# Loading the tokens, the first modulation chunk and the first key weights in longer lines and another order, with a reordered chain to the first normed tokens

## Chip, cores and metric

The kernel runs on one core of a Trainium2 chip. The metric is the device time of one execution in microseconds, the median of three runs.

## What is computed

One layer of a hybrid backbone over 256 latent tokens `x` of 1,024 channels, beside 256 context tokens `ctx`. Two vectors, `c` and `c_ctx`, give each token set its own shift, scale and gate through one weight `mod_w`. Cut to what matters here:

```python
c_act, cctx_act = silu(c), silu(c_ctx)
mod_l = c_act @ mod_w + mod_b          # six parts of 1024: sh1, sc1, g1, sh2, sc2, g2
mod_c = cctx_act @ mod_w + mod_b
hl = rmsnorm(x, norm1_g) * (1 + sc1_l) + sh1_l
hc = rmsnorm(ctx, norm1_g) * (1 + sc1_c) + sh1_c
z_l, z_c = hl @ in_w + in_b, hc @ in_w + in_b      # split into ten parts, keys among them
y_l = (sigmoid(..) * conv_l + sigmoid(..) * attention_l + sigmoid(..) * rnn_l) @ out_w
x = x + g1_l * y_l
x = x + g2_l * moe(rmsnorm(x, norm2_g) * (1 + sc2_l) + sh2_l)     # 16 experts, 2 per token
```

## The kernel before

Channels lie on the partitions: `xl` holds the tokens as 128 partitions x 8 blocks of channels x 256 tokens, `xct` the context in the same way. The projections work in three matmuls per block (`mm3`, lines 68 to 70), a weight and a token block each split into a high and a low part: `wh*xh`, `wh*xl`, `wl*xh`. A weight is loaded into a `raw` tile, its high part made on ScalarE, its low part on VectorE (`split_parts`, lines 201 and 202, in the start; `split`, lines 73 and 74, later).

The start, which the change touches, comes before the first projection, that of the keys. Its steps:

- **Loads**, all from the SyncE queue (`load`, line 78) in program order. At most eight are on their way at a time, since they share eight semaphores. Order: the conditioning `cct`, eight pieces of the tokens and the context in turn (two channel blocks each, lines of 2 KB), the table of small vectors `vc`, then the first modulation chunk in two halves (`load_ma_half`, four loads each, lines of 512 B), with the first key weight `w_k` between the halves; then the next two modulation chunks and key weights.
- **Sums of squares.** ScalarE squares each channel block of the tokens and of the context (lines 244, 245, 371, 372); VectorE adds them up in `sqs`, a part of the tile `nrm` (line 373). Four matmuls with a column of ones make the sums over the partitions (`pst`, line 381).
- **Modulation.** A `Mod` takes one or two blocks of scale and shift: `products` (line 349: small matmuls `mps` of 32 rows over the eight channel blocks), `copy` (ScalarE, line 354), `turn` (line 359, `mpt`) and `finish` (VectorE, `modA` and `modB`, lines 364 and 366). The first chunk goes in two halves, `m0` and `m1`, one channel block each.
- **Root and spread.** `rsqrt` (lines 294 to 305) is ten small VectorE instructions on four columns; `spread` copies the result to 128 columns for each (`ex`, line 312) and transposes it on TensorE (`prs`, line 315), so that it lies along the tokens. ScalarE copies that to `rstd1` (line 389).
- **Normed blocks.** `Channels(k)` scales a block on VectorE (`xn`, line 409), adds the shift and rounds on ScalarE (`h`, line 414), and makes the low part on VectorE (line 418). The first block then meets the first key weight: `kps` (lines 68 to 70).

After it, a loop of three rounds takes two channel blocks a round: 48 key matmuls, the products of the next modulation chunk, the split of the next key weight. The instructions of TensorE, ScalarE and VectorE in this stretch run in the order in which they are written (`manual_schedule`); from there on a scheduler orders them by data. Later come the convolution, the recurrence and the attention, the output projection, the second norm with the router (`rsqrt` again) and the experts, whose weights stream in 512 KB pieces through `ew` tiles as buffers come free.

## Time and profile before

| | |
|---|---|
| median of three runs | 615.6 us (613.79 to 617.37) |
| profiled execution | 619.23 us, its span 617.5 us |
| TensorE busy | 582.8 us (94% of the span) |
| VectorE busy | 349.0 us (57%) |
| ScalarE busy | 259.8 us (42%) |
| GpSimd busy | 19.4 us (3%) |
| moved by DMA | 170.64 MB, mean 276 GB/s |
| granted TensorE clock, mean | 0.997 |

Busy shares are means over the whole span; TensorE's 94% hides that the first slice of the span has almost no work for it. A change in one stage is read from the rows of that stage: which wait ended last there, and what the engines did beside it.

### The profile page before, as it was taken

The numbers are of one execution on the slowest core, as the hardware profiler recorded it, in microseconds if no ns is written. First come the engines' busy times: TensorE is split into PE (matmuls) and PEld (weight loads), VectorE is DVE, ScalarE is ACT, GpSimd is POOL, SyncE is SP. The second block draws the span as 40 slices with busy tenths as digits, with TensorE's granted clock in tenths as the row PEclk, the third lists the DMA queues.
The fourth block names the chain that finished last, engine by engine and source line by source line (L and its number), as shares of the span: only waits on it lengthen the run. The fifth ranks groups of instructions, "written<-read, shape, count | busy, mean of one in ns | idle before, by whom it ended". The sixth has DMA issues, their size and how long they took to land. (4 is left out here: it accounts for less than half of the span.)

```text
span 617.5 us, 10619 instructions
## 1 busy us (share of the span) xinstructions
PE 582.8 (94%) x4127; PEld 408.8 (66%) x4127; DVE 349.0 (57%) x797; ACT 259.8 (42%) x456; POOL 19.4 (3%) x42
## 2 busy tenths in 40 slices
PE   1999989999999899999999988998999999989996
PEld 0789878768788877888899974335444434454364
DVE  4667989999758977988468554120222303132123
ACT  4345436664498855886645634212111211131101
POOL 0000000000000000102212010000000000000000
PEclk9999999999999999999999998999999999999999
DMA  8983965446763373658969875999999999969971
GB/s 253 374 338 114 310 232 170 137 137 186 263 233 103 111 266 102 206 204 331 318 218 368 291 229 218 372 365 394 407 374 407 408 407 409 409 200 411 408 302 68
DMA packets 51824, 170.64 MB, mean 276 GB/s; under 512 B 5664, under 2 KB 10016, under 8 KB 51744
## 3 DMA queue, kind: packets, MB, share of 16 engines
q1 hardware_dynamic: 46704, 151.26, 66.9%
q0 software_dynamic: 5040, 18.35, 8.5%
q8 instruction: 45, 0.74, 0.5%
q14 instruction: 35, 0.29, 0.1%
HBM read 168.54 MB, written 1.05 MB: 275 GB/s over the span
## 5 line engine op out<-in xcount | busy, mean ns | idle before, releaser
L1162 PE MATMUL ph<-ew,xg 128*64 128x512 f32 (+1 forms) x576 | 115.8, 548 | 1.9 <-issue 1.6
L73 ACT ACTIVATE w<-raw 128x1024 fp32r<-128x1024 f32 x68 | 71.8, 1057 | 67.9 <-DMA raw<-in_w_in 12.0
L74 DVE TENSOR_TENSOR w<-raw,w 128x1024 fp32r<-128x1024 f32 x68 | 82.9, 1219 | 24.1 <-ACT w L73 22.5
L1162 PEld LDWEIGHTS ph<-ew,xg 128*64 128x64 f32 x576 | 40.7, 137 | 65.4 <-issue 56.5
L70 PE MATMUL gps<-h,w 128*128 128x256 f32 x192 | 55.2, 288 | 1.1 <-DVE w L74 1.1
L68 PE MATMUL gps<-h,w 128*128 128x256 f32 x192 | 56.0, 292 | 0.4 <-DVE y L934 0.4
L69 PE MATMUL gps<-h,w 128*128 128x256 f32 x192 | 54.5, 284 | 0.0
L593 DVE SCALAR_TENSOR_TENSOR cacc<-up,vc,cacc 128x243 f32<-128x243 f32 (+14 forms) x120 | 52.1, 471 | 1.4 <-ACT cacc L585 0.7
L1183 PE MATMUL py<-ew,heT 128*64 128x512 f32 x224 | 49.6, 595 | 1.2 <-ACT heT L1178 0.8
L1171 DVE SCALAR_TENSOR_TENSOR he<-sl,gsl,ph 128x256 f32<-128x256 f32 x16 | 7.1, 478 | 75.9 <-PE ph L1162 74.9
L74 DVE TENSOR_TENSOR ys<-py,ys 128x512 fp32r<-128x512 f32 (+1 forms) x18 | 11.4, 632 | 58.0 <-ACT ys L73 58.0
L68 PEld LDWEIGHTS gps<-h,w 128*128 128x128 f32 x192 | 36.7, 191 | 4.1 <-issue 2.6
L70 PEld LDWEIGHTS gps<-h,w 128*128 128x128 f32 x192 | 36.7, 191 | 2.8 <-issue 1.5
L69 PEld LDWEIGHTS gps<-h,w 128*128 128x128 f32 x192 | 36.7, 191 | 0.9 <-issue 0.7
L1183 PEld LDWEIGHTS py<-ew,heT 128*64 128x64 f32 x224 | 15.5, 137 | 30.8 <-issue 25.7
L1201 DVE SCALAR_TENSOR_TENSOR xl<-scp,g,xl 128x256 f32<-128x256 f32 x72 | 29.2, 476 | 7.6 <-PE scp L1197 7.6
L73 ACT ACTIVATE ys<-py 128x512 fp32r<-128x512 f32 (+1 forms) x18 | 9.9, 550 | 50.5 <-PE py L1183 36.6
L1167 ACT ACTIVATE sl<-ph 128x512 f32<-128x512 f32 (+1 forms) x9 | 4.9, 550 | 61.1 <-PE ph L1162 38.2
L114 POOL DMA_DIRECT2D ew<-in_w_exp x31 | 16.6, 537 | 323.5 <-ACT pp L813 251.2
L1119 ACT ACTIVATE xg<-gps,b2m 128x256 f32<-128x256 f32 x32 | 13.4, 470 | 24.6 <-PE gps L1115 23.8
L349 PE MATMUL mps<-ma,cs 128*32 128x256 f32 (+1 forms) x160 | 10.1, 397 | 13.4 <-DMA ma<-in_mod_a 13.2
L1115 PEld LDWEIGHTS gps<-oh,hT 128*128 128x128 f32 x128 | 16.2, 194 | 6.8 <-issue 3.7
(358 smaller groups left out, 1313.1 us busy)
## 6 DMA issues: line engine op xcount, KB each, us to landing
ew<-in_w_exp SPq DMA_DIRECT2D x161, 512.0 KB, 10.2
raw<-in_w_in SPq DMA_DIRECT2D x40, 512.0 KB, 4.3
ew<-in_w_exp POOLq DMA_DIRECT2D x31, 512.0 KB, 7.8
raw<-in_mod_b SPq DMA_DIRECT2D x28, 512.0 KB, 4.1
ma<-in_mod_a SPq DMA_DIRECT2D x12, 512.0 KB, 10.1
raw<-in_w_br SPq DMA_DIRECT2D x12, 512.0 KB, 4.2
raw<-in_w_out SPq DMA_DIRECT2D x8, 512.0 KB, 7.7
ma<-in_mod_a SPq DMA_DIRECT2D x8, 256.0 KB, 6.8
```

What stands on the lines that cost most here:

```text
L68: pe.matmul(ps, wh, xh, start=start, stop=False, skip_group_check=True)
L69: pe.matmul(ps, wh, xl_, start=False, stop=False, skip_group_check=True)
L70: return pe.matmul(ps, wl, xh, start=False, stop=stop, skip_group_check=True)
L73: act.activation(hi, src, AF.Copy)
L74: dve.tensor_tensor(lo, src, r32(hi), op=ALU.subtract)
L114: queue.dma_start(t, w_exp[6 * p + 2 * i + s, :, 1024 * q:1024 * q + 1024])
L593: dve.scalar_tensor_tensor(cacc[:, b, i0:i1], up[:, b, i0 + o:i1 + o], half_d[:, b * 31 + j:b * 31 + j + 1], cacc[:, b, i0:i1], op0=ALU.mu ...
L1115: pe.matmul(ps[:, j, :], hT[i][t][:, k * 128:k * 128 + 128], oh[t], start=(j == 0 and t == 0 and i == 0), stop=(t == 1 and i == 1), skip_g ...
L1119: act.activation(place(k0 + j), ps[:, j, :], AF.Identity, bias=b2m[:, k0 + j:k0 + j + 1])
L1162: pe.matmul(ph[64 * s:64 * s + 64, cols], xg(k)[:, c:c + 64], w[:, at], start=k == 0 and not h, stop=k == KD - 1, skip_group_check=True)
L1183: pe.matmul(py[q][64 * s:64 * s + 64, :], heT[f // 2][:, f % 2, 64 * s:64 * s + 64], ew[p][2][f][s][:, q * 512:q * 512 + 512], start=f == ...
L1201: dve.scalar_tensor_tensor(xl[:, m, :], ps[:, j, :], g2[:, m:m + 1], xl[:, m, :], op0=ALU.mult, op1=ALU.add)
```

## The change

**Loads.** The tokens come in pieces of four channel blocks (lines of 4 KB, 512 KB each), the last half of the context in two pieces of two blocks. The first key weight and then the vector table follow the tokens at once. The first modulation chunk is laid out anew on the host, so that each half is two loads of 4 KB lines (`load_ma_half`), and both halves stand together behind them. In the places of SyncE's queue up to the first loads of the second chunk, before:

```order
L78 DMA cct<-in_cc 128x16
L78 DMA xl<-in_x_all 128x512
L78 DMA xc<-in_x_all 128x512
...
L78 DMA vc<-in_vecs 128x318
L78 DMA ma<-in_mod_a 128x4x128 x4
L78 DMA raw<-in_w_k 128x1024
L78 DMA ma<-in_mod_a 128x4x128 x4
L78 DMA ma<-in_mod_a 128x1024 x4
```

and of the change:

```order
L78 DMA cct<-in_cc 128x16
L78 DMA xl<-in_x_all 128x1024
L78 DMA xc<-in_x_all 128x1024
L78 DMA xl<-in_x_all 128x1024
L78 DMA xc<-in_x_all 128x512 x2
L78 DMA raw<-in_w_k 128x1024
L78 DMA vc<-in_vecs 128x318
L78 DMA ma<-in_mod_a 128x1024 x8
```

The key weight moved ahead of the vector table and of both halves of the chunk; nine token and table loads became seven with the weight among them.

**Chain.** Squares and sums work on two blocks of one side at a time (512 columns, `sqa`), each side added up by itself and its two halves added last. On TensorE the four `pst` matmuls stand ahead of all products of `m0`, which were split around them. On VectorE (`nrm` is the tile of the sums, `rq` the root, `w` the low part of the weight, `ex` the spread) the stretch from the last sums to the first scaling was:

```order
L373 TENSOR_TENSOR nrm<-nrm,sq 128x512
L524 TENSOR_SCALAR sc2p<-vc 128x8
L294 TENSOR_SCALAR rq<-pst 128x4
...
L305 SCALAR_TENSOR_TENSOR rq<-rq 128x4
L312 COPY ex<-rq 128x512
L364 TENSOR_SCALAR modA<-mpt,sc1p,vc 128x2
L366 TENSOR_SCALAR modB<-mpt,vc 128x2
L202 TENSOR_TENSOR w<-raw,w 128x1024
L409 SCALAR_TENSOR_TENSOR xn<-xl,modA,nrm 128x256
```

and is now:

```order
L377 TENSOR_TENSOR nrm<-nrm,sq 128x512
L379 TENSOR_TENSOR nrm<-nrm 128x256
L202 TENSOR_TENSOR w<-raw,w 128x1024
L387 TENSOR_SCALAR sc1p<-vc 128x8
L297 TENSOR_SCALAR rq<-pst 128x4
...
L307 SCALAR_TENSOR_TENSOR rq<-rq 128x4
L314 COPY ex<-rq 128x512
L369 TENSOR_SCALAR modA<-mpt,sc1p,vc 128x2
L371 TENSOR_SCALAR modB<-mpt,vc 128x2
L414 SCALAR_TENSOR_TENSOR xn<-xl,modA,prs 128x256
```

The low part of the weight moved from behind the root to ahead of it, the first scaling reads `prs` where it read the copy in `nrm`, and `rsqrt` has one instruction less, in this place and its three others. Five small instructions on the vector table (`half_b`, three on `vc`, `qg8`) moved from ahead of the root to behind the first normed block, `sc2p` behind the last one of the loop.

```diff
-    for i in range(4):
-        load(xl[:, 2 * i:2 * i + 2, :], x_all[0, :, 2 * i:2 * i + 2, :])
-        load(xct[i // 2][:, i % 2 * 2:i % 2 * 2 + 2, :], x_all[1, :, 2 * i:2 * i + 2, :])
-    load(vc, vecs)
+    x_parts = [(i, k, 4) for k in (0, 4) for i in range(2)]
+    x_parts[-1:] = [(1, 4, 2), (1, 6, 2)]
+    for i, k, n in x_parts:
+        load((xct[k // 4][:, k % 4:k % 4 + n, :] if i else xl[:, k:k + n, :]), x_all[i, :, k:k + n, :])
...
+        for q in range(2):
+            load(ma[0][2 * j + q], mod_a[0].rearrange("p (j q k) (s c) -> p (j q) (k s c)", j=2, q=2, s=2)
+                 [:, 2 * j + q, :].rearrange("p (k c) -> p k c", k=4))
...
-    act.activation(sqs[:, 0, :], xl[:, 0, :], AF.Square)
-    act.activation(sqs[:, 1, :], xc(0), AF.Square)
-    load_ma_half(0, 0)
+    for i in range(2):
+        act.activation(sqa[i], x_pair(i, 0), AF.Square)
     load_w()
-    load_ma_half(0, 1)
+    load(vc, vecs)
+    load_ma_half(0)
+    load_ma_half(1)
...
-        dve.tensor_scalar(t.bitcast(I32), x.bitcast(I32), 1, None, op0=ALU.arith_shift_right)
-        dve.tensor_scalar(y_.bitcast(I32), t.bitcast(I32), -1.0, float(0x5f3759df), op0=ALU.mult, op1=ALU.add)
+        dve.tensor_scalar(y_.bitcast(I32), x.bitcast(I32), -0.5, float(0x5f3759df), op0=ALU.mult, op1=ALU.add)
...
-    for k in range(1, KD):
+    for k, i in ((2, 0), (2, 1), (4, 0), (6, 0), (4, 1), (6, 1)):
         sq = work.tile([128, 2, T], F32, tag="sq", name="sq", bufs=NSQ)
-        act.activation(sq[:, 0, :], xl[:, k, :], AF.Square)
-        act.activation(sq[:, 1, :], xc(k), AF.Square)
-        dve.tensor_tensor(sqs, sqs, sq, op=ALU.add)
+        act.activation(sq, x_pair(i, k), AF.Square)
+        dve.tensor_tensor(sqa[i], sqa[i], sq, op=ALU.add)
+        if k == 6:
+            dve.tensor_tensor(sqs[:, i, :], sqa[i][:, 0, :], sqa[i][:, 1, :], op=ALU.add)
...
     m0 = Mod(0, 0)
-    m0.products(range(2))
+    w0 = split_parts()
+    w0[0]()
+    w0[1]()
+    dve.tensor_scalar(sc1p, v("mod_b", 8, 8), 1.0, None, op0=ALU.add)
     pst = ax_bank((128, 4), "pst")
     for t in range(4):
         pe.matmul(pst[:, t:t + 1], sqs[:, t // 2, (t % 2) * 128:(t % 2) * 128 + 128], ones[:, 0:1],
                   start=t == 0, stop=True, skip_group_check=True)
-    m0.products(range(2, 4))
-    w0 = split_parts()
+    m0.products()
     m0.copy()
-    w0[0]()
     m0.turn()
     prs = spread(rsqrt([pst], 4, 1.0 / D), 4, "prs")
-    act.activation(rstd1, prs, AF.Copy)
     m0.finish()
-    w0[1]()
...
-    c.scale()
+    c.scale(prs)
     c.high()
+    act.activation(rstd1, prs, AF.Copy)
     m1.copy()
     c.low()
+    dve.tensor_scalar(half_b, v("in_b", 0, 52), 0.5, None, op0=ALU.mult)
...
```

## Rows read from the trace of the kernel before

**Rows 1.** Busy time by stretches: us, then engines, clock, DMA share, GB/s.

```profile
0.00:20.00 20.00, 5.73 (x46) 4.02 (x46) 9.88 (x40) 8.50 (x20) 0.69 (x7) 1.00 0.91 267
20.00:40.00 20.00, 19.66 (x201) 16.66 (x201) 12.91 (x33) 8.07 (x16) 0.00 (x0) 1.00 1.02 405
```

**Rows 2.** Timeline of the start: start us, us, instruction, [idle before it <- what ended it].

```profile
11.78 0.42 ACT L372 ACTIVATE sq<-xc 128x256 f32<-128x256 f32 x1 [0.97 <-DMA xc<-in_x_all]
...
13.24 1.45 PE L349 MATMUL mps<-ma,cs 128*32 128x128 f32 x16 [13.24 <-DMA ma<-in_mod_a]
...
14.61 1.87 PE L381 MATMUL pst<-ones,nrm 128*128 128x1 f32 x8
...
16.52 0.16 DVE L294 TENSOR_SCALAR rq<-pst 128x4 f32<-128x4 f32 x1 [2.41 <-PE pst L381]
...
18.50 0.43 DVE L312 COPY ex<-rq 128x512 f32<-128x512 f32 x1
...
20.02 1.94 PE L349 MATMUL mps<-ma,cs 128*32 128x128 f32 x32
20.13 0.60 ACT L389 ACTIVATE nrm<-prs 128x512 f32<-128x512 f32 x1 [1.35 <-PE prs L315]
...
21.89 0.58 PE L68 MATMUL kps<-h,w 128*128 128x256 f32 x1
...
22.36 0.29 PEld L69 LDWEIGHTS kps<-h,w 128*128 128x128 f32 x1 [0.18 <-DVE h L418]
```

**Rows 3.** Busy time by stretches again, for the last two columns, DMA.

```profile
2.00:4.00 2.00, 0.00 (x0) 0.00 (x0) 0.35 (x2) 0.24 (x2) 0.00 (x0) 1.00 0.60 186
4.00:6.00 2.00, 0.00 (x0) 0.00 (x0) 0.00 (x0) 0.76 (x3) 0.00 (x0) 1.00 0.95 257
6.00:8.00 2.00, 0.00 (x0) 0.00 (x0) 0.89 (x2) 1.75 (x7) 0.00 (x0) 1.00 0.88 311
8.00:10.00 2.00, 0.00 (x0) 0.00 (x0) 1.90 (x7) 1.59 (x6) 0.00 (x0) 1.00 1.03 314
10.00:20.00 10.00, 5.73 (x46) 4.02 (x46) 6.06 (x25) 2.90 (x7) 0.00 (x0) 1.00 1.12 319
21.00:26.00 5.00, 5.00 (x52) 4.10 (x48) 3.29 (x10) 1.98 (x5) 0.00 (x0) 1.00 1.03 411
```

**Rows 4.** Groups by line: instruction, forms, count | busy us, mean ns | idle before.

```profile
L373 DVE TENSOR_TENSOR nrm<-nrm,sq 128x512 f32<-128x512 f32 x7 | 4.8, 691 | 5.4 <-ACT nrm L245 3.7 <-ACT sq L372 1.5
L202 DVE TENSOR_TENSOR w<-raw,w 128x1024 fp32r<-128x1024 f32 x4 | 4.9, 1222 | 4.1 <-ACT w L201 4.1
L409 DVE SCALAR_TENSOR_TENSOR xn<-xl,modA,nrm 128x256 f32<-128x256 f32 x8 | 3.8, 477 | 0.4 <-ACT nrm L389 0.4
L1201 DVE SCALAR_TENSOR_TENSOR xl<-scp,g,xl 128x256 f32<-128x256 f32 x72 | 29.2, 476 | 7.6 <-PE scp L1197 7.6
```

**Rows 5.** Timeline of the first key matmuls, and VectorE beside them.

```profile
22.95 0.41 PE L68 MATMUL kps<-h,w 128*128 128x256 f32 x1
23.17 0.41 PE L69 MATMUL kps<-h,w 128*128 128x256 f32 x1
...
24.05 0.28 DVE L364 TENSOR_SCALAR modA<-mpt,sc1p,vc 128x2 f32<-128x2 f32 x1 [1.35 <-PE mpt L359]
...
24.20 0.28 PE L70 MATMUL kps<-h,w 128*128 128x256 f32 x1
24.31 0.28 PE L68 MATMUL kps<-h,w 128*128 128x256 f32 x1
```

**Rows 6.** Timeline of the first round of the loop.

```profile
27.28 1.06 ACT L201 ACTIVATE w<-raw 128x1024 fp32r<-128x1024 f32 x1 [1.48 <-DMA raw<-in_w_k]
...
28.66 0.61 PE L359 MATMUL mpt<-fold,mrow 128*128 128x4 f32 x4 [0.34 <-ACT mrow L354]
```

**Rows 7.** Timeline of TensorE at the router.

```profile
371.59 0.18 PE L1084 MATMUL pk<-maskb,tri 128*128 128x16 bf16 x1 [2.84 <-DVE maskb L1061]
```

**Rows 8.** Waits of the weight loads in the expert stage: us in total, times, longest us.

```profile
PEld ph L1162 <- DMA ew<-in_w_exp: 2.8, 10, 0.3
```

More of the change, by code (lines that the diff above doesn't have):

```diff
@@ L221, in load_ma, with load_ma_half @@
             load(ma[i][q], mod_a[i, :, 2 * q:2 * q + 2, :])
-    def load_ma_half(i, j):
+    def load_ma_half(j):
         if j == 0:
-            ma.append([cut(piece(name="ma"), 0, [2, 512]) for _ in range(4)])
-        for q in range(4):
-            x = mod_a[i, :, 2 * q:2 * q + 2, :].rearrange("p k (s c) -> p k s c", s=2)
-            t = ma[i][q].rearrange("p k (s c) -> p k s c", s=2)
-            load(t[:, :, :, 128 * j:128 * j + 128], x[:, :, :, 128 * j:128 * j + 128])
+            ma.append([cut(piece(name="ma"), 0, [4, 256]) for _ in range(4)])
+        for q in range(2):
+            load(ma[0][2 * j + q], mod_a[0].rearrange("p (j q k) (s c) -> p (j q) (k s c)", j=2, q=2, s=2)
+                 [:, 2 * j + q, :].rearrange("p (k c) -> p k c", k=4))
     xct = [cut(piece(name="xc"), 0, [4, T]) for _ in range(2)]
-    for i in range(4):
-        load(xl[:, 2 * i:2 * i + 2, :], x_all[0, :, 2 * i:2 * i + 2, :])
-        load(xct[i // 2][:, i % 2 * 2:i % 2 * 2 + 2, :], x_all[1, :, 2 * i:2 * i + 2, :])
-    load(vc, vecs)
+    x_parts = [(i, k, 4) for k in (0, 4) for i in range(2)]
+    x_parts[-1:] = [(1, 4, 2), (1, 6, 2)]
+    for i, k, n in x_parts:
+        load((xct[k // 4][:, k % 4:k % 4 + n, :] if i else xl[:, k:k + n, :]), x_all[i, :, k:k + n, :])
     def xc(k):
@@ L241, in tile_kernel, with x_pair @@
     nrm = piece(name="nrm")
+    sqa = [cut(nrm, 512 * i, [2, T]) for i in range(2)]
     sqs = cut(nrm, 0, [2, T])
     rstd1 = cut(nrm, 512, [512])
-    act.activation(sqs[:, 0, :], xl[:, 0, :], AF.Square)
-    act.activation(sqs[:, 1, :], xc(0), AF.Square)
-    load_ma_half(0, 0)
+    def x_pair(i, k):
+        return xct[k // 4][:, k % 4:k % 4 + 2, :] if i else xl[:, k:k + 2, :]
+    for i in range(2):
+        act.activation(sqa[i], x_pair(i, 0), AF.Square)
     load_w()
-    load_ma_half(0, 1)
+    load(vc, vecs)
+    load_ma_half(0)
+    load_ma_half(1)
     for i in (1, 2):
@@ L325, in tile_kernel @@
     sc1p = pers.tile([128, KD], F32, name="sc1p")
-    dve.tensor_scalar(sc1p, v("mod_b", 8, 8), 1.0, None, op0=ALU.add)
     modA = pers.tile([128, KD, 2], F32, name="modA")
@@ L347, in products @@
                     for s in range(2):
-                        c, o = 32 * (2 * j + s), 256 * s + self.o
-                        pe.matmul(self.ps[c:c + 32, :], cs[:, 2 * n + j, :], ma[self.i][n][:, j, o:o + self.w],
-                                  start=n == 0, stop=n == KD // 2 - 1, skip_group_check=True)
+                        c, k = 32 * (2 * j + s), 2 * n + j
+                        if self.w == 256:
+                            x = ma[self.i][n][:, j, 256 * s:256 * s + 256]
+                        else:
+                            x = ma[0][self.o // 64 + k // 4][:, k % 4, 128 * s:128 * s + 128]
+                        pe.matmul(self.ps[c:c + 32, :], cs[:, k, :], x, start=n == 0, stop=n == KD // 2 - 1,
+                                  skip_group_check=True)
         def copy(self):
@@ L480, in tile_kernel @@
     c = Channels(0)
-    c.scale()
+    c.scale(prs)
     c.high()
+    act.activation(rstd1, prs, AF.Copy)
     m1.copy()
     c.low()
+    dve.tensor_scalar(half_b, v("in_b", 0, 52), 0.5, None, op0=ALU.mult)
+    for x in (half_d, half_r, half_l):
+        dve.tensor_scalar(x, x, 0.5, None, op0=ALU.mult)
+    dve.tensor_scalar(qg8, v("qg"), 0.125, None, op0=ALU.mult)
     load_w()
@@ L523, in tile_kernel @@
     sc2p = pers.tile([128, KD], F32, name="sc2p")
-    dve.tensor_scalar(sc2p, v("mod_b", 32, 8), 1.0, None, op0=ALU.add)
+    with tc.issue_after(last_k.last_dve.ins):
+        dve.tensor_scalar(sc2p, v("mod_b", 32, 8), 1.0, None, op0=ALU.add)
     def mod_round_b(out, bank):
@@ L1469, in layout @@
     sh1, sc1 = mw[:, :, 0:1024], mw[:, :, 1024:2048]
-    d["mod_a"] = C(np.stack([np.concatenate([sc1[:, :, 256 * i:256 * i + 256], sh1[:, :, 256 * i:256 * i + 256]],
-                                            axis=2) for i in range(4)]))
+    ma = [np.concatenate([sc1[:, :, 256 * i:256 * i + 256], sh1[:, :, 256 * i:256 * i + 256]], axis=2)
+          for i in range(4)]
+    ma[0] = ma[0].reshape(128, KD, 2, 2, 128).transpose(0, 3, 1, 2, 4).reshape(128, KD, 512)
+    d["mod_a"] = C(np.stack(ma))
     d["mod_b"] = C(np.stack([mw[:, :, 2048:4096].transpose(1, 0, 2), mw[:, :, 4096:6144].transpose(1, 0, 2)]))
```

8 lines of the change are left out of this document (2 added, 6 removed).

## Prediction

> **What bounds the kernel now.** I read the busy time by stretches first [rows 1]: TensorE works 5.73 us of the first 20 and 19.66 of the next 20, so what the change can reach is the start, up to the first projection matmul of the keys (`kps`). Then the timeline of the start [rows 2]: TensorE's first work waits 13.24 us for a tile of the modulation; the last piece of the tokens is squared from 11.78, its wait ended by a DMA; the sums' matmuls `pst` run from 14.61, the inverse root `rq` from 16.52 to 18.50 in ten instructions (0.2 us each), then the spreading copy `ex` (0.43), its transposes `prs`, sixteen modulation products of the second half (32 records, 1.94 us from 20.02) and `kps` at 21.89. The copy of `prs` to SBUF (0.60, from 20.13) and the first scaling run beside those products. So the chain is: tokens land, squares and sums, root, spread, products, `kps`. From there TensorE hardly idles, and a microsecond won ahead of 21.89 should reach the end unless something later is timed by another engine.
>
> The third view is the load stream by stretches [rows 3]. With token lines of 2 KB it moves 186, 257 and 311 GB/s from 2 to 8 us, and 319 from 10 to 20, where most lines are of 512 B, at a busy share of 1.12. From 21 to 26 us, with lines of 4 KB, it moves 411 at 1.03.
>
> **The change part by part.**
>
> *When the tokens are there.* Up to the last token piece, conditioning and tokens are 8 + 2,097 KB. The rows give 2 x (186 + 257 + 311 + 314) = 2,136 KB by 10 us, and the piece is used at 11.78, some 1.9 later. The change gives the tokens the 4 KB lines (but for the last two pieces). No row shows such lines in the first 8 us, so I bound this. Fast end: 411 GB/s from 2.0 us, 5.1 us, and 1.5 until use: 8.6. Slow end of this case: the shares of the rows from 2 to 8 stay (0.60, 0.95, 0.88) at 411/1.03 = 399 GB/s per full share: 479 + 758 + 702 = 1,939 KB by 8 us, the rest by 8.4, and 1.9 until use: 10.3. Slowest of all: the old pace, 11.5. I take 9.5, the middle of the first two, because the pieces now have the shape of those of 21 to 26 us. The rows thus speak for a pace that goes with the line: 319 at 512 B and 411 at 4 KB, the engines full in both. The Trainium skill (DMA: Bandwidth & Descriptors, Specifications) puts line rate at transfers of 512 B and up. By that rule the longer lines would win nothing, and the sum would be that of the first rival below; the two paces speak against it.
>
> *From there to the root.* The third of the pieces lands some 1.3 us (512 KB at 411) ahead of the last. Its first square takes about 0.6 (nearest row: the 128x512 copy, 0.60 [rows 2]), so VectorE starts 0.65 us ahead of the last piece on four adds of 0.69 [rows 4] and two sums of halves, below 0.48 each (nearest row of 256 columns: `L409`): 3.7 us, to 3.0 us after the last piece. New there, ahead of the root on VectorE, is the low part of the first weight split (`L202`, 1.22 [rows 4]) and one small instruction (0.2). The split waits for ScalarE's high part, which needs the weight piece, 1.3 us behind the tokens, and about 1.1 us: 2.4, below 3.0, so it does not wait. The root starts at 4.45; the four `pst` matmuls (14.61 to 16.52 before, half of them now done early) take about 1 us beside the split, so moving the split ahead costs some 0.4. Nine root instructions instead of ten: 1.8. The spread: 0.43. End: 6.7 us after the last piece, or 16.2. The first modulation half lands 1.3 + 0.4 (the vector table) + 2.6 = 4.3 after it; its last products, copy and turn take another 1.5 or so, so it is not the later one.
>
> *From the spread to the keys.* 18.50 + 0.43 = 18.93 to 21.89 is 2.96 us, the transposes and the second half's products, both unchanged; that half lands 6.9 after the last piece, before the transposes end. Reading `prs` in place takes a 0.60 copy out of the way of the scaling, but `kps` waits for the products on TensorE itself: nothing for the first matmul. The second waits less, about 0.2 (a wait of 0.18 on `h` [rows 2]). The scaling now reads PSUM: the instruction of the same size that does so (`L1201`) takes 476 ns against 477 [rows 4], so I add nothing. `kps` starts at 9.5 + 6.7 + 2.96 = 19.15, a gain of **2.75 us**.
>
> *Behind it.* The five small VectorE instructions moved behind the first normed block, about 0.8 us, fall in an idle stretch of 1.35 there [rows 5]; without it they would delay the second block by as much. The second key weight was used as it landed, at 27.28, the modulation copy queued behind it on ScalarE, and TensorE then waited 0.34 for it at 28.66 [rows 6]. Counted on from 9.5, it lands 1.3 + 0.4 + 5.1 + 5.1 + 1.3 = 13.2 later, at 22.7, against a need at 19.15 + 5.4 = 24.5: that wait and the copy's delay go, about **0.5**. With the **0.25** of the second matmul the first stage wins 3.5. What is late next there is the next modulation chunk, which stands just ahead of that weight in the queue and lands 1.3 ahead of it, at 21.4.
>
> *Far behind.* The root at the second norm loses one instruction of 0.2; TensorE stands there 2.84 us for the mask that is made from it [rows 7]: **0.2**. The other two roots lie beside matmuls: nothing. The expert weights' DMAs start when buffers come free, and so move with TensorE; the ten waits of the product's weight loads for them are 0.3 us at the longest [rows 8].
>
> **Sum:** 2.75 + 0.25 + 0.5 + 0.2 = 3.7 us. The profiled execution took 619.23 (span 617.5 and 1.7 around it), so 615.5 by its own time. It lies 3.6 above the median of the runs shown, 615.6; from that the sum gives **611.9**. A half per cent, about what a measurement of this kernel can tell from no change, is 3.1 us.
>
> **The rivals.**
>
> *The longer lines buy nothing.* The early pace is then set by something else, and the bytes move as before. For it: from 2 to 4 us the share is 0.60, so the engines lacked work rather than speed. Against it: at full share the rows differ by line (319 and 411). The last token is used at 11.5, `kps` at 11.5 + 6.7 + 2.96 = 21.15; 0.7 + 0.95 = 1.65 won: **614.0**.
>
> *The start's gain is given back.* TensorE comes early and waits for what did not: a weight piece, VectorE's taps, the expert stream. For it: the second key weight had no slack at all [rows 6], and weight loads in the expert stage do wait for a DMA [rows 8]. Against it: every later transfer waits for a buffer that TensorE or VectorE frees, so it moves along, and the sum above leaves slack for the first pieces. Only the 0.2 stays: **615.4**.
>
> *TensorE's clock.* This one ends slower. The first `kps` matmuls follow each other at 0.21 us and the later ones at 0.12 [rows 5], 256 columns at 1.2 and at 2.4 GHz, though the granted clock stands at 1.00 in all of these stretches; the faster pace comes at 24 us, after TensorE had worked without a wait from the second half's products on. If the new order, which leaves TensorE idle between the sums and the products, holds that level back, each matmul of 192 costs 0.095 more. It eats the gain at 39 more slow matmuls, and 72 make it slower by half a per cent: **618.7**. Against it: from the transposes to `kps` TensorE's work is the same and as dense as before. The Trainium skill (TensorE: Matmul & The Clock Gate, Part 1) has the array at half rate after idling and at full rate after sustained work; the two paces of rows 5 agree with it, and no row tells how the new gap counts.
>
> **How the numbers follow.** My forecast has 0.63. Its own ends, tokens at 8.6 or 10.3, give 611.0 and 612.7, so some 0.08 of it lies within half a per cent. No gain from long lines 0.18, given back 0.13, the clock 0.06. Faster by over 0.5%: 0.55; within: 0.08 + 0.18 + 0.13 = 0.39; slower: 0.06. Three runs of before spread by 3.6 us, so a median may be off by about 1 to 1.5. The range goes from 609.4 (fast end, less that) to 615.0 (the first rival, and 1 more); it leaves out most of the given-back case and the clock.
>
> **What would show it.** The last token squared by about 9.5 instead of 11.78; 512 KB pieces landing 1.3 us apart from the start; the low split ahead of the root without a wait for ScalarE; `kps` near 19.2; no wait of TensorE on the modulation copy in the first round; the later stages shifted as one. I am wrong in the early pace if the tokens are late, wrong in the chain if `kps` comes more than 10 us behind them, and wrong in the carrying-over if `kps` is early and the end is not.

## The result and the profile after

The changed kernel took **611.74 us** (median of nine runs, 611.03 to 613.22), the kernel before 617.12 beside it (nine runs, 613.79 to 618.62). The ratio is 0.9934, its 95% interval 0.9912 to 0.9957: faster by 2.7 to 5.4 us. The forecast was 611.9, in a range from 609.4 to 615.0. The profiled execution took 612.92, its span 611.1. (Of the kernel with 512 B lines below, one run of twelve, 661.34 us at a granted clock of 0.853, is left out of the ratio.)

The busy time by stretches, first what answers to [rows 1], then to [rows 3]:

```profile
0.00:20.00 20.00, 7.80 (x80) 6.06 (x81) 11.65 (x42) 9.20 (x16) 0.69 (x7) 1.00 0.87 325
20.00:40.00 20.00, 20.00 (x208) 17.36 (x211) 13.99 (x36) 8.27 (x15) 0.00 (x0) 1.00 1.00 394
2.00:4.00 2.00, 0.00 (x0) 0.00 (x0) 0.35 (x2) 0.24 (x2) 0.00 (x0) 1.00 0.84 301
4.00:6.00 2.00, 0.00 (x0) 0.00 (x0) 0.31 (x1) 1.15 (x2) 0.00 (x0) 1.00 0.76 203
6.00:8.00 2.00, 0.00 (x0) 0.00 (x0) 0.38 (x1) 1.08 (x2) 0.00 (x0) 1.00 0.92 331
8.00:10.00 2.00, 0.00 (x0) 0.00 (x0) 1.80 (x6) 1.22 (x4) 0.00 (x0) 1.00 1.03 374
10.00:20.00 10.00, 7.80 (x80) 6.06 (x81) 8.13 (x27) 4.25 (x8) 0.00 (x0) 1.00 1.03 408
```

TensorE works 2.07 us more in the first 20 us. From 10 to 20 us the stream moves 408 GB/s where it moved 319, as forecast. From 2 to 8 it moves 301, 203 and 331 against 186, 257 and 311: 1,670 KB against 1,508, far from the 411 of 4 KB lines later.

The timeline of the start, answering to [rows 2] and [rows 5]:

```profile
10.79 0.63 ACT L376 ACTIVATE sq<-xc 128x512 f32<-128x512 f32 x1 [0.17 <-DVE nrm L377]
...
11.75 2.07 PE L390 MATMUL pst<-ones,nrm 128*128 128x1 f32 x8 [11.75 <-DVE nrm L379]
12.33 0.42 DVE L379 TENSOR_TENSOR nrm<-nrm 128x256 f32<-128x256 f32 x1
12.68 1.22 DVE L202 TENSOR_TENSOR w<-raw,w 128x1024 fp32r<-128x1024 f32 x1
...
13.88 0.15 DVE L297 TENSOR_SCALAR rq<-pst 128x4 f32<-128x4 f32 x1
...
15.66 0.43 DVE L314 COPY ex<-rq 128x512 f32<-128x512 f32 x1
...
16.18 0.59 PE L364 MATMUL mpt<-fold,mrow 128*128 128x4 f32 x2 [0.40 <-ACT mrow L359]
...
16.63 1.09 PE L317 MATMUL prs<-ident,ex 128*128 128x128 f32 x4
...
17.66 1.94 PE L354 MATMUL mps<-ma,cs 128*32 128x128 f32 x32
17.77 0.48 DVE L414 SCALAR_TENSOR_TENSOR xn<-xl,modA,prs 128x256 f32<-128x256 f32 x1 [0.55 <-PE prs L317]
...
19.52 0.58 PE L68 MATMUL kps<-h,w 128*128 128x256 f32 x1
...
20.29 0.28 PE L68 MATMUL kps<-h,w 128*128 128x256 f32 x1
```

The last token piece landed at 10.19 (before: 11.75) and was squared from 10.79, held by a buffer that VectorE's adds had to free. The low split (`L202`) lies beside the sums' matmuls, which run to 13.82, and ends with them. The spread copy ends at 16.09, but `prs` starts at 16.63, behind the modulation's turn `mpt`. The keys start at 19.52, 2.37 earlier.

The timeline of the first round and of the router, the waits of the weight loads, and a group by line, answering to [rows 6], [rows 7], [rows 8] and [rows 4]:

```profile
23.64 1.06 ACT L201 ACTIVATE w<-raw 128x1024 fp32r<-128x1024 f32 x1 [0.86 <-DMA raw<-in_w_k]
...
25.08 0.55 PE L364 MATMUL mpt<-fold,mrow 128*128 128x4 f32 x4
...
366.51 0.18 PE L1095 MATMUL pk<-maskb,tri 128*128 128x16 bf16 x1 [2.63 <-DVE maskb L1072]
```
```profile
PEld ph L1173 <- DMA ew<-in_w_exp: 3.4, 12, 0.3
```
```profile
L414 DVE SCALAR_TENSOR_TENSOR xn<-xl,modA,nrm 128x256 f32<-128x256 f32 x7 | 3.3, 478 | 0.0
```

The second key weight is still used as it lands, but `mpt` no longer waits. At the router the wait is 0.21 shorter. Reading `prs` in PSUM took 0.48, reading the copy in SBUF 0.478.

From 28 to 82 us ScalarE's instructions stand 3.64 earlier than before (the splits of weights, which wait for a load, 2.9 to 3.6); towards the end it is 6.2 to 6.3. Nearly all of the difference comes at two places far behind, some 1.1 each, near 84 us and at the router, and the first experiment below shows that they belong to the profiled execution of before, not to the change.

### The profile page after: what moved, and what is told of

Read it like the earlier page. It is cut to its first block, busy times and chain, and to the rows that moved or that the text cites. A ratio compares the mean times of both kernels' runs of the same rounds, so it can differ in the third digit from the quotient of the medians.

```text
span 611.1 us, 10594 instructions
## 1 busy us (share of the span) xinstructions
PE 580.3 (95%) x4127; PEld 407.4 (67%) x4127; DVE 348.2 (57%) x794; ACT 258.9 (42%) x448; POOL 19.4 (3%) x42
## 5 line engine op out<-in xcount | busy, mean ns | idle before, releaser
L1130 ACT ACTIVATE xg<-gps,b2m 128x256 f32<-128x256 f32 x32 | 13.4, 471 | 24.4 <-PE gps L1126 23.5
L1208 PEld LDWEIGHTS scp<-oT,ys 128*128 128x128 f32 x128 | 15.7, 188 | 6.7 <-issue 5.2
```

The source lines that it names most:

```text
L1208: pe.matmul(ps[:, j, :], rows_(i, m), toks(m), start=(j == 0 and i == 0), stop=i == parts - 1, skip_group_check=True)
```

## Experiments

The table gives, from each profiled execution: when the last token piece landed; the first key matmul; the first one that the next follows at the fast pace (within 0.16 us, and at 0.12 from there); when the second key weight landed; and when the last key matmul ended, after which TensorE's work is the same in all of them. The ratio is to runs of the kernel before beside it (9 to 12 runs against 9 to 35). The times are those of one execution each, and executions differ: the first experiment, whose loads are those of before, had its last token 0.6 earlier by chance. So small differences between rows of the table count only where the trace shows a reason.

| kernel | last token | first keys | fast pace | second weight | keys end | ratio (95% interval) |
|---|---|---|---|---|---|---|
| before | 11.75 | 21.89 | 24.08 | 27.26 | 54.50 | 1 |
| **change** | 10.19 | 19.52 | 20.29 | 23.62 | 50.85 | 0.9934 (0.9912 to 0.9957) |
| root only | 11.14 | 21.16 | 21.90 | 26.50 | 53.73 | 0.9995 (0.9974 to 1.0016) |
| loads only | 10.22 | 21.77 | 22.63 | 23.57 | 53.27 | 1.0005 (0.9988 to 1.0022) |
| chain only | 11.73 | 24.45 | 25.05 | 26.73 | 55.70 | 1.0038 (1.002 to 1.0056) |
| tokens in 2 KB lines | 11.93 | 21.35 | 23.44 | 25.46 | 53.27 | 0.9989 (0.997 to 1.0008) |
| modulation in 512 B lines | 10.24 | 20.10 | 22.83 | 26.92 | 55.63 | 1.0027 (1.0009 to 1.0044) |
| low split late | 10.40 | 19.56 | 22.82 | 23.65 | 52.01 | one run |
| scaling from the copy | 10.31 | 19.61 | 20.40 | 23.57 | 51.03 | one run |
| TensorE kept busy | 10.00 | 18.07 | 18.82 | 24.36 | 51.59 | 1.0038 (1.0015 to 1.006) |
| the same, round reordered | 10.49 | 18.22 | 18.96 | 24.94 | 53.34 | 1.0038 (1.0015 to 1.0062) |
| 64 instructions earlier | 10.26 | 19.41 | 21.71 | 24.48 | 51.70 | 1.0015 (0.9984 to 1.0046) |
| two queues | 9.32 | 21.63 | 24.57 | 22.70 | 53.90 | 0.9989 (0.9962 to 1.0017) |
| two queues, second try | 11.10 | 20.36 | 23.51 | 22.93 | 52.70 | 0.9973 (0.9952 to 0.9994) |

**The shorter root alone**, in the kernel before.

```diff
-        dve.tensor_scalar(t.bitcast(I32), x.bitcast(I32), 1, None, op0=ALU.arith_shift_right)
-        dve.tensor_scalar(y_.bitcast(I32), t.bitcast(I32), -1.0, float(0x5f3759df), op0=ALU.mult, op1=ALU.add)
+        dve.tensor_scalar(y_.bitcast(I32), x.bitcast(I32), -0.5, float(0x5f3759df), op0=ALU.mult, op1=ALU.add)
```

> The kernel before with nothing but the shorter root (nine instructions in place of ten, in all four places). Theory: the keys start 0.2 us earlier and the second norm saves 0.2, so 0.4 in all (ratio 0.9993), no change that can be measured; the waits for the first w_rx weight near 84 us (1.57 on ScalarE) and the router's modulation products at half pace (2.6 us for the 24 matmuls) stay as they were. Rival, that the two savings far behind the start (some 1.2 us at 84, 1.1 at the router) come by chance and not from the earlier start: one or both of them show up here too, and the ratio falls to 0.998 or below.

No measurable change in time, as expected. Its profile is the telling part: the span is 612.6, 4.9 less than that of before. The last token happened to land 0.61 earlier (the keys ended 0.77 earlier), and both places far behind that I had seen in the change's profile show up here too. Before, one of them is a wait on ScalarE at 84 us (its timeline):

```profile
84.48 1.06 ACT L73 ACTIVATE w<-raw 128x1024 fp32r<-128x1024 f32 x1 [1.57 <-DMA raw<-in_w_rx]
```

It is gone in both. The other is the router: TensorE's timeline and the stretch from 365 to 375, of before and then with the root alone:

```profile
371.80 2.61 PE L532 MATMUL mps<-late,cs 128*32 128x256 f32 x24
```
```profile
365.00:375.00 10.00, 7.15 (x83) 4.18 (x84) 7.06 (x39) 3.32 (x7) 0.38 (x1) 0.85 1.01 359
```
```profile
368.50 1.50 PE L531 MATMUL mps<-late,cs 128*32 128x256 f32 x24
```
```profile
365.00:375.00 10.00, 6.91 (x69) 3.66 (x58) 7.96 (x36) 4.71 (x10) 0.00 (x0) 1.00 0.95 362
```

Granted clock 0.85 in the one, 1.00 in the other, and 1.11 us on 24 matmuls. So these steps separate two executions, not two kernels; the profile of before, at 619.23, was a long one. The rival of the expectation, chance, holds for them, though the ratio did not fall with them as it said. What the change is worth is read at the end of the keys: 54.50 against 50.85, **3.65 us**, within the measured 2.7 to 5.4. It is one execution against one, and good to some 0.6.

**The loads alone**, with the old chain.

```diff
-    load_ma_half(0, 0)
     load_w()
-    load_ma_half(0, 1)
+    load(vc, vecs)
+    load_ma_half(0)
+    load_ma_half(1)
```

(with the change's token pieces and layout of the first modulation chunk)

> The kernel before with the change's loads alone (token pieces of 4 KB lines, key weight and vector table behind them, the modulation halves in 4 KB lines), and the old chain. Theory, that loads and chain need each other: the old chain puts half of the first modulation products ahead of the sums, and that piece lands at 13.4; so the sums run from about 14.4 to 16.2, the root ends near 18.3, and the keys start near 21.6, 0.3 earlier than before; the first round then still saves 1.2, and what lies far behind up to 2: a ratio from 0.9975 to 0.994. The kernel with the whole change then stays 1.5 to 2 us ahead. Rival, that the loads carry the whole gain: keys at 19.5 to 19.8 and a ratio of 0.9934. Rival, that the chain carries it: ratio 1.000.

The tokens came as in the change, and no time was won: 1.0005, where 0.994 to 0.9975 was expected. TensorE's timeline shows why:

```profile
13.48 1.08 PE L353 MATMUL mps<-ma,cs 128*32 128x128 f32 x16 [13.48 <-DMA ma<-in_mod_a]
14.49 1.87 PE L385 MATMUL pst<-ones,nrm 128*128 128x1 f32 x8
```

Half of the modulation products stand ahead of the sums and wait for a piece that lands later than the tokens. `pst` starts at 14.49, where it did before (14.61). The keys start at 21.77; only the first round saved its 1.1, so that the keys ended 1.23 earlier, and the runs do not show even that.

**The chain alone**, with the old loads: the change's code, with the token pieces, the order and the two modulation halves of before.

```diff
+    load(vc, vecs)
...
+    load_ma_half(0, 0)
     load_w()
-    load(vc, vecs)
-    load_ma_half(0)
-    load_ma_half(1)
+    load_ma_half(0, 1)
```

> The changed kernel with the old loads (pieces of 2 KB lines, modulation halves of 512 B lines on either side of the key weight). Theory: the low part of the split stands ahead of the root and now waits for a weight that lands at 17.1; the high part takes 1.1, the low 1.22, the root 1.8, the spread 0.43, then 3.0 to the keys: 24.7, 2.8 later than before; the first round gives back some 1, so the end is 1.5 to 3 us later than before, a ratio of 1.002 to 1.005. Rival, that the chain carries a part of the gain by itself: keys at 21 or earlier, a ratio of 0.998 or below.

Slower, by the wait that was forecast (the timeline of ScalarE and VectorE):

```profile
16.99 1.06 ACT L201 ACTIVATE w<-raw 128x1024 fp32r<-128x1024 f32 x1 [4.09 <-DMA raw<-in_w_k]
18.08 1.23 DVE L202 TENSOR_TENSOR w<-raw,w 128x1024 fp32r<-128x1024 f32 x1 [3.84 <-ACT w L201]
...
19.30 0.15 DVE L297 TENSOR_SCALAR rq<-pst 128x4 f32<-128x4 f32 x1
```

The root stands behind a split of a weight that lands late. By the end of the keys the new loads alone win 1.23 and the new chain alone loses 1.20, and neither shortens the runs; together they win 3.65. The gain belongs to the pair: the order of the loads is the order in which the chain uses them.

**Tokens in 2 KB lines**, all else as in the change.

```diff
-    x_parts = [(i, k, 4) for k in (0, 4) for i in range(2)]
-    x_parts[-1:] = [(1, 4, 2), (1, 6, 2)]
+    x_parts = [(i, k + h, 2) for k in (0, 4) for i in range(2) for h in (0, 2)]
```

> The changed kernel with its tokens in eight pieces of 2 KB lines, in the change's order; all else as in the change. Theory, that the token stream goes by the length of the lines: the last piece lands at 11.4 to 11.8 as in the kernel before (changed kernel: 10.2), the keys start at 20.7 to 21.1, and the ratio to the kernel before is 0.996. Rival, that the tokens' early pace is set by something else and that the change's gain there comes from what was moved behind them: last piece by 10.4, keys at 19.5 to 19.8, ratio 0.9934.

The last piece landed 1.74 later than in the change, everything behind it too, and the keys ended 2.42 later (some 0.5 of it by a later step to the fast pace, of which more below). The ratio, 0.9989, is nearer to before than expected. So the shape of the token pieces (line length, and with it eight pieces instead of five; the run does not part the two) is worth more than half of the gain. It is not the pace of the stream alone: from 2 to 10 us this kernel moves 259, 192, 354 and 335 GB/s, 2,280 KB, against 2,418 in the change. That is more than the 2,105 KB up to the last token, and still that piece landed only at 11.93. A piece lands with the slowest of the engines that carry it. Each load ends with sixteen completion events in the trace: of that piece, fifteen had come by 10.39 and the last came at 11.93 (in the change 10.18 and 10.19). Nor is it the line at full pace: a packet of 2 KB took 84 ns and one of 4 KB 159 (medians), some 6% more for the same bytes. What made one engine lag, no run tells; but the last piece landed at 11.14 to 11.93 in the four kernels with these 2 KB pieces and at 10.00 to 10.49 in the eight with the change's pieces on one queue.

**The modulation halves in 512 B lines**, in the change's place.

```diff
-    load_ma_half(0)
-    load_ma_half(1)
+    load_ma_half(0, 0)
+    load_ma_half(0, 1)
```

> The changed kernel with the two halves of the first modulation chunk in the old layout (eight loads of 512 B lines), in the change's place behind the key weight. Theory: by the old pace of some 0.88 us for 256 KB the first half lands at 15.5 and the second at 19.1, so the first keys start no more than 0.3 later than the 19.5 of the changed kernel, because TensorE is busy till then anyway; but everything behind it in the queue lands 1.8 to 2 later, the next chunk at 24.2 and the second key weight at 25.5, and in the first round TensorE waits for the modulation copy behind that weight: 1.2 to 1.8 of the first round's gain is lost, ratio 0.9955 to 0.997. Rival, that these lines do not matter: weight at 23.6, ratio 0.9934.

Worse than either side expected: the whole gain is lost. The first keys came 0.58 late, but the second weight 3.3, and TensorE waited for the copy queued behind it (the timeline, then the stretches):

```profile
26.94 1.06 ACT L201 ACTIVATE w<-raw 128x1024 fp32r<-128x1024 f32 x1 [3.12 <-DMA raw<-in_w_k]
...
28.32 0.61 PE L361 MATMUL mpt<-fold,mrow 128*128 128x4 f32 x4 [1.61 <-ACT mrow L356]
```
```profile
10.00:20.00 10.00, 7.49 (x78) 5.36 (x78) 7.57 (x24) 3.74 (x7) 0.00 (x0) 1.00 1.16 327
...
26.00:28.00 2.00, 0.71 (x6) 0.50 (x5) 0.00 (x0) 1.06 (x2) 0.00 (x0) 1.00 1.04 416
...
30.00:32.00 2.00, 2.00 (x11) 2.00 (x11) 1.82 (x5) 0.91 (x2) 0.00 (x0) 0.50 1.05 412
32.00:34.00 2.00, 2.00 (x15) 2.00 (x14) 1.42 (x4) 1.49 (x3) 0.00 (x0) 0.73 1.01 404
```

From 10 to 20 us the stream moves 327 GB/s at a full share where the change moves 408. The lines differ, and with them the pieces (eight instead of four); that it is the lines show the packets, of which one of 512 B took 33 ns and one of 4 KB 159 (medians), five times as long for eight times the bytes. The Trainium skill (DMA: Bandwidth & Descriptors, Specifications) has line rate from 512 B on; this trace disagrees (327 against 408). TensorE was idle for most of 26 to 28 us and worked again from 28.32, and then its granted clock fell to 0.50 (1.2 GHz), and some 15 key matmuls followed each other at 0.21 instead of 0.12, until 32.9: 1.4 us. A late weight costs its wait and then the clock. The step to the fast pace, at 22.83 instead of 20.29, took some 0.7 more, which has no tie to the weight. Of the weight's 3.3 us, 1.3 were not the lines'; the experiment on the instruction stream below tells whose. So the lines' own part of the loss was not measured by itself.

**The low split late**, behind the root as before.

```diff
     w0[0]()
-    w0[1]()
...
     m0.finish()
+    w0[1]()
```

> The changed kernel with the low part of the first weight split back behind the root, where it stood. Theory, as the prediction had it, that it costs 0.4 ahead of the root: the root starts up to 0.4 nearer to the last sum. Rival, that it lies wholly beside the four matmuls of the sums, which end when it ends: the root starts as late behind the last sum as in the changed kernel (1.13 us), and the split then delays the first scaling by 1.2 and the second key matmul by some 0.5, the first by 0 to 0.2.

The timeline of VectorE and TensorE:

```profile
13.84 0.16 DVE L297 TENSOR_SCALAR rq<-pst 128x4 f32<-128x4 f32 x1 [1.10 <-PE pst L389]
17.17 1.22 DVE L202 TENSOR_TENSOR w<-raw,w 128x1024 fp32r<-128x1024 f32 x1
...
18.30 0.47 DVE L414 SCALAR_TENSOR_TENSOR xn<-xl,modA,prs 128x256 f32<-128x256 f32 x1
...
19.56 0.58 PE L68 MATMUL kps<-h,w 128*128 128x256 f32 x1
```

The rival holds: VectorE waits 1.10 for `pst`, the root starts 1.1 behind the last sum as in the change, and neither place of the split moves the first key matmul. My 0.4 for it was nothing. (The keys ended 1.16 later because the fast pace came only at 22.82, of which more below.)

**The scaling from the copy**, as before.

```diff
-    c.scale(prs)
+    c.scale()
     c.high()
-    act.activation(rstd1, prs, AF.Copy)
```

(the copy stands ahead of `m0.finish`, where it stood before)

> The changed kernel with the first scaling reading the copy of the spread root in SBUF as before, and ScalarE's copy ahead of it. Theory, as predicted, that reading in place wins nothing for the first key matmul and 0.25 for the second: the scaling starts 0.6 later behind the transposes, the first key matmul at the end of the products as now, the second 0.2 to 0.4 later. Rival: the first key matmul too comes 0.3 to 0.6 later, because the normed block and not the products sets it.

The first key matmul is 0.09 later, but the transposes `prs` start 0.09 later already (16.72), so reading in place is worth nothing there. The second follows 0.47 behind it instead of 0.38. The theory holds, and the 0.2 to 0.4 that it gave the second was 0.1.

**TensorE kept busy** from 1 us on.

```diff
+    warm = ax_bank((128, 128), "warm")
+    for x, n in ((ones, 8), (xl[:, 0, 0:T // 2], 10), (xc(0)[:, 0:T // 2], 7), (xl[:, 4, 0:T // 2], 4),
+                 (xc(4)[:, 0:T // 2], 4), (xc(6)[:, 0:T // 2], 6)):
+        for _ in range(n):
+            pe.matmul(warm, ones, x, start=True, stop=True, skip_group_check=True)
     m0 = Mod(0, 0)
```

> The changed kernel with 39 matmuls on TensorE ahead of the sums, on ones and on token pieces as they land; nothing reads what they make (38 to 39 more matmuls, the output unchanged). Theory, that TensorE's level in the start is a matter of what it did before: with it working from 1 us on, the sums' matmuls, the transposes, the products of the second half and the first key matmuls run at the faster pace from the start; the transposes take 0.55 in place of 1.09, the products 1.0 in place of 1.94 but not before their last piece lands at 17.2: keys at 17.8 to 18.2 in place of 19.5. Of that the first round gives nearly all back, because the modulation copy stands behind the second key weight, which lands at 23.6: the stretch behind 28 us is 0 to 0.7 earlier than in the changed kernel. Rival, that the level does not depend on it: keys at 19.5 and the pace of 0.21 until 20.3.

The timeline:

```profile
16.33 0.63 PE L317 MATMUL prs<-ident,ex 128*128 128x128 f32 x4 [0.57 <-DVE ex L314]
16.89 1.08 PE L354 MATMUL mps<-ma,cs 128*32 128x128 f32 x32
18.07 0.39 PE L68 MATMUL kps<-h,w 128*128 128x256 f32 x1
...
24.39 1.06 ACT L201 ACTIVATE w<-raw 128x1024 fp32r<-128x1024 f32 x1 [2.93 <-DMA raw<-in_w_k]
...
25.77 0.61 PE L364 MATMUL mpt<-fold,mrow 128*128 128x4 f32 x4 [1.09 <-ACT mrow L359]
```

The level is a matter of what TensorE did before (working from 1 us on, it was at the higher clock from 6.93): transposes 0.63 instead of 1.09, products 1.08 instead of 1.94, keys at 18.07. But the second weight landed 0.74 later than in the change, TensorE waited for it, and the whole lead was gone at 25.77 (the change: 25.08). By the end of the keys it was 0.74 behind, and the time was 1.0038, far worse than that.

**The same with the round reordered**: the copy ahead of the next weight's high part, the low part behind the first normed block.

```diff
         m.products()
-        w[0]()
         m.copy()
-        w[1]()
+        w[0]()
         k_block(2 * i, 3)
         m.turn()
         m.finish()
         channels(2 * i + 2)
+        w[1]()
         last_k = channels(2 * i + 3)
```

> As the one with 39 more matmuls ahead of the sums, and in the three rounds the modulation copy stands ahead of the high part of the next weight, the low part behind the first normed block of the round. Theory: what the second key weight took back in the first round stays won, 1.2 to 1.8 more than the changed kernel from 28 us on, a ratio of 0.9905. Rival, that the first round is held by something else (the next chunk, landing at 22.3, or VectorE): less than 0.5 more, ratio 0.993.

Neither: the tokens landed 0.3 later than in the change, the last piece of the next chunk was late (TensorE waited 0.64 for it) and then the low part of the weight (two waits of 0.6, VectorE's, which the new order put later). The keys ended 2.49 later than in the change. With TensorE faster, the first round is bound by the loads and the splits that stand behind them.

**64 instructions earlier.** Why was the second weight late with TensorE kept busy, though all that was loaded was the same? In the change, pieces landed 1.28 apart, but the one after 23.62 only at 26.19, and at 23.64 the trace has one packet of 16 KB on the instruction queue q8. The DMA queues from 23.6 to 24.8 (packets, MB, share of 16 engines):

```profile
q1 hardware_dynamic: 128, 0.48, 99.5%
q8 instruction: 1, 0.02, 5.4%
```

5.4% of 16 engines in 1.2 us is 1.03 us on one engine. A piece is spread over the engines, and one that is a microsecond behind makes every later piece late: of the piece of 26.19, fifteen of the sixteen completions had come by 24.89. With TensorE kept busy the packet came at 16.75, with the 512 B lines at 24.39, ahead of the weight in both. This kernel moves it alone:

```diff
+    early = ax_bank((128, 4), "early")
+    for _ in range(16):
+        pe.matmul(early[:, 0:1], ones, ones[:, 0:1], start=True, stop=True, skip_group_check=True)
     m0 = Mod(0, 0)
```

> The changed kernel with 16 matmuls of one column on ones at the very start, long before the tokens; nothing reads them. Their only lasting effect is that TensorE is 64 instructions further in its stream (16 matmuls, two passes each with a weight load) at every later point. Theory: in the changed kernel the second key weight landed at 23.62, 0.02 ahead of a 16 KB packet of the instruction queue that held one DMA engine for 1.03 us and made the next weight piece 1.29 late; that packet comes when TensorE reaches a place in its stream, so it now comes at 21 to 22.4, ahead of the weight, which lands at 24.9; TensorE waits 1 to 1.3 for the modulation copy behind it; the keys start at 19.5 as before, and what is behind 28 us is 1.2 later, or some 3 more if the wait lowers TensorE's clock as in the kernel with the old modulation lines: ratio 0.9955, or 0.999 to 1.001 with the clock. Rival, that the packet has nothing to do with the late pieces: weight at 23.6, ratio 0.9934.

Its DMA queues at that moment and its timeline:

```profile
q8 instruction: 1, 0.02, 5.7%
```
```profile
21.50 0.40 PE L69 MATMUL kps<-h,w 128*128 128x256 f32 x1
...
24.50 1.06 ACT L201 ACTIVATE w<-raw 128x1024 fp32r<-128x1024 f32 x1 [1.37 <-DMA raw<-in_w_k]
...
25.88 0.61 PE L364 MATMUL mpt<-fold,mrow 128*128 128x4 f32 x4
```

The packet came at 19.91, and the long gap between pieces moved with it (19.66 to 22.09). The second weight landed at 24.48, 0.86 late. The rival, that the packet has nothing to do with the late pieces, falls. In all fourteen profiles this packet comes when TensorE has 220 to 278 recorded instructions behind it, and the next one at 464 to 498, whatever the time. The keys ended 0.85 late, but not by the weight alone: `mpt` stood behind the copy, which ended at 25.82, and TensorE, whose fast pace came at 21.71 instead of 20.29, was 0.62 late by itself; the 1 to 1.3 that I expected it to wait did not show. The time, 1.0015, is some 5 us above the change's; 0.85 explains a sixth. In this profile most of the rest is one wait of TensorE in the expert stage, put down to no releaser (the timeline):

```profile
543.90 1.32 PE L1129 MATMUL gps<-oh,hT 128*128 128x256 f32 x5 [4.55 <-issue]
```

An 8 KB packet of the other instruction queue ends 0.18 ahead of it. Behind the wait the granted clock falls to 0.50, which costs some 1.2 more. In the kernel with TensorE kept busy 2.5 us are lost to late expert weights (`ew`) near 465 us. All three kernels that add matmuls are slower than the end of their keys says, and the other timed ones agree with it to 0.003. Their runs also show a lower granted clock than those of before beside them (means of 0.993 to 0.994 against 0.997 to 0.998), and in this kernel the time goes with it, from 612.33 at 1.000 to 620.57 at 0.988; yet the tokens in 2 KB lines have 0.9945 without such a loss. That waits far behind, and the clock after them, come from the shift of TensorE's instruction stream is argued, not shown: no run isolated which fetch or load it meets there.

**Two queues.** Is the slow early pace that of one queue?

```diff
-        load((xct[k // 4][:, k % 4:k % 4 + n, :] if i else xl[:, k:k + n, :]), x_all[i, :, k:k + n, :])
+        (nc.scalar if (i, k) in ((1, 0), (0, 4)) else nc.sync).dma_start((xct[k // 4][:, k % 4:k % 4 + n, :] if i else xl[:, k:k + n, :]), x_all[i, :, k:k + n, :])
```

(the later squares and sums come under the manual order as well)

> The changed kernel with two of the five token pieces (the first of the context, the second of the tokens) issued from ScalarE's queue, the others and all later loads from SyncE's as they were. Theory, that the early pace is held by the one queue (301, 203 and 331 GB/s from 2 to 8 us against 409 later): with two, the last token lands at 8.9 to 9.4 instead of 10.2, and keys, weights and the end all move by the same 0.8 to 1.3: ratio 0.9915. Rival, that the early pace is the memory's or the engines' own: last token at 10 to 10.4, keys at 19.3 to 19.8, ratio 0.9934; a loss is possible if the pieces now land in another order than they are squared in.

The stretches, and ScalarE's first square:

```profile
2.00:4.00 2.00, 0.00 (x0) 0.00 (x0) 0.00 (x0) 0.95 (x1) 0.00 (x0) 1.00 0.81 214
4.00:6.00 2.00, 0.00 (x0) 0.00 (x0) 0.35 (x2) 0.22 (x1) 0.00 (x0) 1.00 0.94 352
6.00:8.00 2.00, 0.00 (x0) 0.00 (x0) 0.00 (x0) 0.16 (x1) 0.00 (x0) 1.00 1.02 403
```
```profile
7.84 0.63 ACT L251 ACTIVATE nrm<-xl 128x512 f32<-128x512 f32 x1 [3.37 <-DMA xl<-in_x_all]
```

Half right. 1,938 KB move from 2 to 8 us instead of 1,670, and every load lands 0.9 earlier. But the queues share the engines: the context's first piece lands at 5.19, the two pieces of the tokens only at 7.82 and 8.07, and the squares begin with the tokens. The first starts at 7.84 instead of 4.51, and eight squares then stand in a row: keys 2.11 later.

**Two queues, second try**: the context in four pieces from ScalarE's queue, the tokens in two from SyncE's, squares in the order of landing.

```diff
-    x_parts = [(i, k, 4) for k in (0, 4) for i in range(2)]
-    x_parts[-1:] = [(1, 4, 2), (1, 6, 2)]
+    x_parts = [(1, 0, 2), (0, 0, 4), (1, 2, 2), (0, 4, 4), (1, 4, 2), (1, 6, 2)]
...
-        load((xct[k // 4][:, k % 4:k % 4 + n, :] if i else xl[:, k:k + n, :]), x_all[i, :, k:k + n, :])
+        (nc.scalar if i else nc.sync).dma_start((xct[k // 4][:, k % 4:k % 4 + n, :] if i else xl[:, k:k + n, :]), x_all[i, :, k:k + n, :])
```

(all squares and sums under the manual order, in the order (0, 1), (2, 1), (0, 0), (2, 0), (4, 1), (4, 0), (6, 0), (6, 1) of block and side, side 1 the context)

> The changed kernel with the context in four pieces of 2 KB lines issued from ScalarE's queue beside the two token pieces of 4 KB lines from SyncE's, and the squares in the order in which such pieces should land. Theory, that two queues fill the early pace (in the first try every load landed 0.9 earlier) and that the first try lost by the order alone (its first two pieces landed together at 7.8 to 8.1): the first square at about 5, the last token at 9.3 to 9.6, the root at 13.2 to 13.5 instead of 13.9, the keys at 18.9 to 19.2 and all later loads 0.5 to 0.9 earlier; ratio 0.992 to 0.993, a version as good as the change or better. Rival: SyncE's pieces still land late beside the second queue, the squares wait, and the keys start at 20 or later: ratio 0.996 or above.

The rival: the first piece landed at 4.11, the next two only at 6.96 and 7.13, and the last at 11.10, behind the weight, which by then shared SyncE's queue. 0.9973, between before and the change. No version that I ran beats the change.

## Why the prediction held, and where it did not

*Total.* The first stage was put at 3.5 us and gave 3.65 by the end of the keys. The sum is right, and several of its terms are not. Two of the errors, late tokens and shorter adds, belong together, as the next paragraphs show. That the other two cancel, keys 0.37 later than forecast and 0.53 more won behind them, is luck. So is a median only 0.2 from the forecast: the forecast counted from 615.6, and the runs of before beside the change had 617.12.

*When the tokens are there.* I took 9.5 for the square of the last piece; it was 10.79. The step that failed is the choice of "the middle of the first two, because the pieces now have the shape of those of 21 to 26 us". The slow end, which keeps the early shares, gave 10.3 and was nearer. 512 KB pieces land 1.3 apart only from 13.4 on (the second came 2.4 behind the first). Landing was 1.56 earlier, not 2.3.

*From there to the root.* The root started at 13.88, 3.1 after that square; I had 4.45, and so 13.95. The adds were mis-sized: the last sum ended 1.96 after that square, not 3.0. VectorE worked without a gap from 9.27, on the third piece, to 12.75, 3.5 us (I had 3.7 from 8.85). So the root hung on the third piece, landed at 8.52, and the late last one, whose square even waited for VectorE's buffers, cost it nothing. And "moving the split ahead costs some 0.4" was nothing: the second half of the sums' matmuls took the 1.0 that I gave them, from 12.81 to 13.82 (the first half ran beside the last adds), and the root came 1.13 behind the last sum with the split ahead of it and 1.1 without, as the kernel with the late split shows. I had added the split and the small instruction end to end, 1.42. From 13.88 to 16.09 the root and spread took 2.21, as forecast (2.23).

*The modulation.* "It is not the later one" is wrong: its turn, not the spread, is what `prs` had to follow, by some 0.5. The last piece of that half landed at 14.66, and products, copy and turn took 2.1 from there, where I had 1.5.

*From the spread to the keys.* 16.63 to 19.52 is 2.89 (forecast from 18.93 to 21.89: 2.96, with the wait). Right, and reading `prs` in place was worth nothing for the first matmul, as forecast, and 0.1 for the second, where I had 0.25.

*Behind it.* 0.75 forecast, 1.28 found. The wait for the copy went, as said. Of the rest, some 0.4 is that TensorE reached its fast pace after 3 slow steps from one key matmul to the next instead of 7, at 0.095 each, and the other profiles have 2 to 12 without a pattern by order. That part counts as luck. The weight landed at 23.62 against a forecast 22.7.

*Far behind.* 0.2 at the router: 0.21. The other roots: nothing seen.

*Rivals.* That longer lines buy nothing fell with the tokens in 2 KB lines, as far as lines can be told from the number of pieces there. That the start's gain is given back did not come true, but by little: the copy behind the second weight ended at 24.98, and `mpt` came at 25.08. With the 512 B lines the change lost everything. I had put the danger in "a weight piece" and given it slack. The clock: the mechanism is real (kept busy, TensorE starts the keys 1.45 earlier, 0.2 of it by earlier tokens; let idle in the first round, it falls to half), but in this execution the change's new gap did not hold it back. That "the granted clock stands at 1.00 in all of these stretches" was a misreading: the trace's record of the clock begins only at the step, at 23.88 before and 20.23 in the change, and ahead of it the views print 1.00 for want of a record.

## What to carry to other kernels

A new load order and a new chain have to be tested as a pair: each alone won nothing or lost here, since an engine that runs in order waits at the first thing that lands late (TensorE at 13.48 with the new loads alone, VectorE at 18.08 with the new chain alone). Before a small wait is called harmless, look at what is queued behind it: a copy behind a weight made TensorE idle, and the idle time lowered its clock, for another 1.4 us. And one profiled execution can differ from another by 5 us in places that the change doesn't touch, so read a start's gain where the start ends, not at the end of the span, and know that the start, too, differs from one execution to the next.

## What I had not expected of the hardware

- Instructions come over the same DMA engines as the data: one 16 KB packet held one engine for 1.03 us, and the pieces of the load stream behind it landed 1.0 to 1.3 later in the change and six of the experiments, 0.2 to 0.85 in before and five, and no later in the one with the tokens in 2 KB lines, where one engine was already 1.4 behind the other fifteen. When it comes goes by TensorE's place in its stream: 64 instructions more ahead moved it 3.7 us forward.
- Early in the program the load stream does not reach its later pace: 203 GB/s from 4 to 6 us with 4 KB lines on one queue, 352 with two (but 214 from 2 to 4, where one had 301), and 408 from 10 us on.
- A load is there when the slowest of its sixteen shares is. Of the last token piece that share came 0.2 to 1.5 us behind the next slowest in the four kernels with 2 KB pieces, and at most 0.4 behind in the eight with the change's pieces on one queue.
- TensorE's first key matmuls run at 0.21 us for 256 columns and then at 0.12. The step is its clock, from 1.2 to 2.4 GHz: in the twelve kernels that do not keep TensorE busy, the trace's record of the granted clock begins within 0.2 us of it, and at 6.93 and 7.07 in the two that do. It comes 0.6 to 3.3 us after the first of them, in kernels whose TensorE did nearly the same before. What sets the moment stays open.
